# A decoder trunk whose engine orders are drawn up on the scheduler's time line model in place of its default model

## The chip, the cores and the metric

The kernel runs on one core of one Trainium2 chip. The metric is the time of one execution on the device in microseconds (us), the median of several runs. Beside it there is one profiled execution, taken by the hardware profiler, from which all rows of traces come.

## The reference

The reference is a trunk of two decoder layers on 256 tokens of width 1024, in float32. Each layer is a feed-forward half step, a mixer, and another feed-forward half step; every stage adds to the residual stream `h`:

```
for layer in range(2):
    h = h + 0.5 * swiglu(rmsnorm(h, ffn1_norm), w_gate, w_up, w_down)     # 1024 -> 2816 -> 1024
    hn = rmsnorm(h, mix_norm)
    h = h + (mixer_a(hn, qkv, w_o) if layer == 0 else mixer_b(hn, w_q, w_o, shared k and v))
    h = h + 0.5 * swiglu(rmsnorm(h, ffn2_norm), ...)
    if layer == 0: shared = k and v of rmsnorm(h, kv_norm)
return rmsnorm(h, final_norm)

swiglu(h) = (silu(h @ w_gate) * (h @ w_up)) @ w_down
```

Both mixers are attention with 16 heads of 64 and a rotary embedding on 16 of the 64 dimensions. Mixer a merges three dilated causal windows, which on 256 tokens comes to one softmax with a mask that counts how often a key is seen. Mixer b is block-sparse, and with 256 tokens in one block of 256 it is plain causal attention.

## The kernel before

**Numbers.** Each float32 operand is split into a high and a low part of type fp32r: the high part is a copy by ScalarE (ACT; `wh`, L156, L307, and L94 for activations), the low part is what is left, a subtraction by VectorE (DVE; `wl`, L157, L309, and L90/L92 for activations). TensorE (PE) multiplies high by high, high by low and low by high. All weights, 174 MB, are streamed from memory once by DMAs that SyncE (SP) issues, into four raw buffers (`rawp`); the parts go into eight buffers for each of `wh` and `wl`.

**Stages.** `ffn("f10")`, mixer a, `ffn("f20")`, `ffn("f11")`, mixer b, and `f21`, whose down projection is written by `down_last`. The first feed-forward has an `opening` (L162 to L174) that brings in the weights and the input in small pieces. In a feed-forward, `products_t` (L193, L196) makes gate and up, `close` (L352 to L356) activates them, `down_t` multiplies by the down weights. `Norm` sums squares (L226 and L229 on ACT, L230 on GpSimd, POOL) and ends in a column of factors (`finish`, L235 on PE).

**A mixer.** `projections` multiplies the normed input by the q, k and v weights (`product`, L182, L184, L186) in six segments. Beside it stand the steps of attention, which go by pairs of heads, 0 to 7:
- the projected q and k are evacuated (L612), rotated (L485 to L488), turned by PE (`qt`, L601) and split into `qkh` and `qkl`;
- scores (`s_a3` is pair 3 of mixer a; L506, two heads on two halves of the array), the masked minimum on DVE (L514), exponentials on ACT (L520), a reciprocal (L525) and a scaling (L527; on POOL, for the last two pairs on DVE);
- turn: the weights of attention are transposed by PE (`pt`, L532) and split into `pT`, high part on ACT (L94), low part on DVE (L90);
- values: `po` (L546, L548) from `pT` and `vs` (L92, L94), evacuated half by ACT (L550) and half by an add on DVE (`o`, L555), and split again into `oT`.

At the end `out_t` (L453 to L455) multiplies the eight `oT` by the output weights into four accumulators, and adds them to the stream `hT` (L472); `norm.scale` then makes the next stage's `x`. PSUM has five accumulators (`accp`), of which `out_t` holds four, and three buffers for transposes and scores (`trp`); `pT` has two buffers.

**What sets the order.** The author writes the program in an order that an `Agenda` works out by hand-given costs and due times: each projection step counts 0.68, each output step 0.72, and a step of attention is written when its due time has come. For the last pairs, for example:

```
def ending(at):
    return [(at + 2.6 * i + wait, step, 4 + i) for i in range(4) for wait, step in ((0.0, "t"), (2.3, "v"))]
```

The rest is left to the framework: inside `tile.TileContext` a scheduler takes the written program with its dependences and decides in which order each engine gets its instructions, by a model of what each of them costs. Engines then run their own lists in order and wait for each other by semaphores. The change is in the call that opens this context:

## Time and profile before

| | |
|---|---|
| median of 3 runs | 990.88 us (990.67 to 990.91) |
| the profiled execution | 990.92 us |
| its span (first to last instruction) | 989.1 us |
| time around the span | 1.8 us |
| granted TensorE clock, mean | 1.00 |
| PE busy | 976.2 us of 989.1 |
| DVE, ACT, POOL busy | 729.4, 586.1, 170.1 us |
| read from memory | 173.99 MB, 177 GB/s over the span |

In rows of the trace the first number is the start in us after the span's start, the second the duration; then come the engine, the line of the kernel, the operation, the tiles (out<-in), the shape, and in brackets the idle time before it and the instruction that ended it. PE's matmuls overlap, so two neighbours are told apart by their starts, not by their durations. In groups of instructions the busy total and the mean in ns stand behind the first bar, the idle time ahead of the group behind the second.

### The profile page before, as it was taken

Reading aid. Unit: us, or ns where it says so; the run is one execution under the profiler, and the core shown is the slowest. Engines: PE = TensorE matmul, PEld = TensorE weight load, DVE = VectorE, ACT = ScalarE, POOL = GpSimd, SP = SyncE. Lnnn points to the kernel's source line nnn. Section 1 sums busy time; section 2 is a strip of 40 time slices with the busy share of each in tenths; the row PEclk is TensorE's granted clock in tenths of the full one; section 3 lists DMA queues with packets and bytes.
Section 4 is the critical chain, followed back from the end, with each engine's and each line's share of the span. In section 5 each row is a group of like instructions: output and inputs, shape, how many; then the busy total and the mean of one; then the engine's idle time right before and its main releaser. Section 6 shows DMA issues by size and latency. Waiting matters only on the chain.

```text
span 989.1 us, 15227 instructions
## 1 busy us (share of the span) xinstructions
PE 976.2 (99%) x5652; PEld 849.5 (86%) x5652; DVE 729.4 (74%) x1291; ACT 586.1 (59%) x1073; POOL 170.1 (17%) x194
## 2 busy tenths in 40 slices
PE   8999999999999999999999999999999999999997
PEld 5888888888889888888888888888888998888886
DVE  6987866677887788776678877656678878888642
ACT  7656654467776665655456566545577756665531
POOL 3211111122302211110112111101143022111000
PEclk9999999999999999999999999999999999999999
DMA  9776565655433566565655665665534345655611
GB/s 303 246 256 204 169 210 185 213 171 171 128 117 125 171 187 206 178 200 181 212 171 172 198 191 185 202 202 190 194 128 128 120 141 173 207 174 201 202 62 43
DMA packets 152395, 176.03 MB, mean 178 GB/s; under 512 B 3584, under 2 KB 140288, under 8 KB 152320
## 3 DMA queue, kind: packets, MB, share of 16 engines
q1 hardware_dynamic: 151600, 174.24, 55.1%
q8 instruction: 44, 0.72, 0.3%
q10 hardware_dynamic: 720, 0.82, 0.2%
q14 instruction: 31, 0.25, 0.1%
HBM read 173.99 MB, written 1.05 MB: 177 GB/s over the span
## 4 chain that ended last, share of the span: by engine, by line
PE 68%; DVE 2%; ACT 2%; issue 1%; POOL 0%; POOLq 0%; ACTq 0%; DVEq 0%
PE f_g L193 12%; PE f_u L193 12%; PE dn_f L193 8%; PE f_u L196 6%; PE f_g L196 6%; PE dn_f L196 4%; PE dn_f_d L186 2%; PE dn_f_d L182 2%; PE dn_f_d L184 2%; PE q_b L182 1%; PE kv_b L182 1%; PE q_b L186 1%; PE kv_b L186 1%; PE kv_b L184 1%; PE q_b L184 1%
## 5 line engine op out<-in xcount | busy, mean ns | idle before, releaser
L193 PE MATMUL f_g<-x_n,wh_f_g 128*128 128x512 f32 x688 | 180.1, 394 | 0.0
L193 PE MATMUL f_u<-x_n,wh_f_u 128*128 128x512 f32 x688 | 177.3, 390 | 0.0
L193 PEld LDWEIGHTS f_u<-x_n,wh_f_u 128*128 128x128 f32 x688 | 129.1, 188 | 27.3
L193 PEld LDWEIGHTS f_g<-x_n,wh_f_g 128*128 128x128 f32 x688 | 124.1, 189 | 22.7
L355 POOL TENSOR_TENSOR j_f_u<-j_f_u,r_n 128x256 f32<-128x256 f32 x88 | 77.6, 884 | 377.9 <-DVE j_f_u L337 355.5
L193 PE MATMUL dn_f<-act_f,wh_f 128*128 128x512 f32 x528 | 126.5, 391 | 0.0
L157 DVE TENSOR_TENSOR wl_f_u<-raw_f_u,wh_f_u 128x1024 fp32r<-128x1024 f32 x86 | 119.6, 1393 | 1.5 <-ACT wh_f_u L156 1.4
L157 DVE TENSOR_TENSOR wl_f_g<-raw_f_g,wh_f_g 128x1024 fp32r<-128x1024 f32 x86 | 103.6, 1235 | 15.1 <-PE f_g L196 10.7
L193 PEld LDWEIGHTS dn_f<-act_f,wh_f 128*128 128x128 f32 x528 | 96.8, 188 | 18.6
L157 DVE TENSOR_TENSOR wl_f<-raw_f,wh_f 128x1024 fp32r<-128x1024 f32 x72 | 81.8, 1153 | 35.6 <-ACT wh_f L156 26.7
L196 PE MATMUL f_u<-x_n,wl_f_u 128*128 128x256 f32 x688 | 103.3, 283 | 0.0
L196 PE MATMUL f_g<-x_n,wl_f_g 128*128 128x256 f32 x688 | 102.9, 282 | 0.0
L196 PEld LDWEIGHTS f_g<-x_n,wl_f_g 128*128 128x128 f32 x688 | 96.5, 190 | 6.3
L156 ACT ACTIVATE wh_f<-raw_f 128x1024 fp32r<-128x1024 f32 x72 | 67.3, 979 | 49.4 <-PE dn_f L193 27.1
L156 ACT ACTIVATE wh_f_g<-raw_f_g 128x1024 fp32r<-128x1024 f32 x86 | 89.4, 1049 | 11.2 <-issue 6.0
L156 ACT ACTIVATE wh_f_u<-raw_f_u 128x1024 fp32r<-128x1024 f32 x86 | 86.6, 1047 | 15.2 <-PE f_g L193 10.9
L196 PEld LDWEIGHTS f_u<-x_n,wl_f_u 128*128 128x128 f32 x688 | 91.6, 192 | 0.0
L230 POOL TENSOR_TENSOR ss_n<-ss_n,sq_n 128x256 f32<-128x256 f32 x42 | 41.9, 999 | 244.2 <-ACT sq_n L229 243.3
L94 ACT ACTIVATE act_f<-j_f_g 128x256 fp32r<-128x256 f32 x88 | 36.5, 417 | 72.1 <-DVE j_f_g L356 71.8
L353 ACT ACTIVATE j_f_g<-j_f_g 128x256 f32<-128x256 f32 x88 | 36.8, 418 | 67.1 <-DVE j_f_g L352 66.6
L196 PEld LDWEIGHTS dn_f<-act_f,wl_f 128*128 128x128 f32 x528 | 68.1, 191 | 2.8
L196 PE MATMUL dn_f<-act_f,wl_f 128*128 128x256 f32 x528 | 69.0, 283 | 0.0
(220 smaller groups left out, 1702.3 us busy)
## 6 DMA issues: line engine op xcount, KB each, us to landing
raw_f_g<-in_ffn_w_gate_dram SPq DMA_DIRECT2D x43, 1024.0 KB, 5.4
raw_f_u<-in_ffn_w_up_dram SPq DMA_DIRECT2D x43, 1024.0 KB, 5.3
raw_f<-in_ffn_w_down_dram SPq DMA_DIRECT2D x24, 1024.0 KB, 5.1
raw_f_d<-in_ffn_w_down_dram SPq DMA_DIRECT2D x11, 1024.0 KB, 4.9
raw_f<-in_ffn_w_down_dram SPq DMA_DIRECT2D x12, 768.0 KB, 4.5
raw_qka<-in_a_w_qkv_dram SPq DMA_DIRECT2D x16, 512.0 KB, 4.3
raw_va<-in_a_w_qkv_dram SPq DMA_DIRECT2D x4, 1024.0 KB, 5.1
raw_ao<-in_a_w_o_dram SPq DMA_DIRECT2D x4, 1024.0 KB, 4.9
```

The source lines that it names most:

```text
L94: nc.scalar.activation(hi, src, AF.Copy, scale=scale)
L156: nc.scalar.activation(wh, r, AF.Copy)
L157: nc.vector.tensor_sub(wl, r, wh.bitcast(F32))
L182: nc.tensor.matmul(ac, xh, wh, start=first, stop=False)
L184: nc.tensor.matmul(ac, xh, wl, start=False, stop=False)
L186: nc.tensor.matmul(ac, xl, wh, start=False, stop=last)
L193: nc.tensor.matmul(ac, wh, flat(x), start=first and i == 0, stop=False)
L196: nc.tensor.matmul(ac[:, :S], wl, x[:, 0, :], start=False, stop=last and i == len(ws) - 1)
L230: nc.gpsimd.tensor_tensor(self.ss, self.ss, sq, op=ALU.add)
L353: nc.scalar.activation(g, g, AF.Silu)
L355: nc.gpsimd.tensor_tensor(u, u, norm.row, op=ALU.mult)
```

## The change

```
@@ -756,7 +756,7 @@
-    with tile.TileContext(nc) as tc:
+    with tile.TileContext(nc, schedule_with_timeline_sim=True) as tc:
         trunk(tc, args, out)
```

The scheduler draws up the orders on its time line model, where it used its default model. The written program is the same, and so are the instructions; what differs is the order on each engine. In the built programs, POOL's order is the same in both. On SP, only the three late constants' loads (L137 to L139) move: from behind the eighth weight load of the first feed-forward and later to a place between the loads of `raw_f10_g2` and `raw_f10_u2`. PE, DVE and ACT differ in the opening, in both mixers and where the next feed-forward begins; in the steady feed-forward and down stages PE's order is the same and a few weight splits swap places. In the mixers, projections stand earlier and steps of attention later and more scattered:

| on PE, both mixers | before | after |
|---|---|---|
| uninterrupted groups of scores (L506) | 16 | 31 |
| matmuls of scores that stand as a pair of heads | 96 pairs | 41 pairs, 110 single |
| groups of values (L546, L548) | 18 | 35 |
| groups of transposes (L532, L601) | 34 | 45 |

At the end of mixer a, DVE's built order after the change is as follows; mixer b has the like:

```
L525 Reciprocal ls_a7
L527 TensorScalarPtr sm_a7_1 (2 instructions)
L157 TensorTensor wl_f20_g0_0<-raw_f20_g0,wh_f20_g0_0
L157 TensorTensor wl_f20_g0_4<-raw_f20_g0,wh_f20_g0_4
L157 TensorTensor wl_f20_u0_0<-raw_f20_u0,wh_f20_u0_0
L157 TensorTensor wl_f20_u0_4<-raw_f20_u0,wh_f20_u0_4
L90 TensorTensor pT_a5_0<-pt_a5_0,pT_a5_0
L555 TensorTensor o_a4<-po_a4,o_a4 (2 instructions)
L90 TensorTensor pT_a5_1<-pt_a5_1,pT_a5_1
L90 TensorTensor oT_a4<-o_a4,oT_a4
```

In `out_t`'s part of PE's order, the last four `oT` (4 to 7) stand after the change with all 24 matmuls each, one `oT` behind the other; before, each accumulator takes the last three `oT` together, 18 matmuls, before the next one does.

## The prediction

> **What bounds the kernel now.** I read the page first, then the waits of TensorE (PE), then busy time by stage, and last the time lines of single stretches.

> ```profile
> span 989.1 us, 15227 instructions
> ...
> PE 976.2 (99%) x5652; PEld 849.5 (86%) x5652; DVE 729.4 (74%) x1291; ACT 586.1 (59%) x1073; POOL 170.1 (17%) x194
> ...
> PEclk9999999999999999999999999999999999999999
> ```

> PE is busy 99% of the span, at a full granted clock throughout. So the end can move in three ways only: PE waits more or less, its matmuls follow each other less or more tightly, or its clock falls. The multiset of PE work is unchanged by this change. The waits of PE and its busy time by stage say how much there is to win:

> ```profile
> PE f_g L193 <- ACT wh L171: 1.7, 2, 1.0
> PE po_a L546 <- DVE vs_a L92: 1.5, 1, 1.5
> ...
> PE po_b L546 <- DVE pT_b L90: 1.0, 1, 1.0
> ```

> ```profile
> 0.00:25.00 25.00, 20.89 (x96) 14.56 (x97) 16.23 (x24) 18.52 (x32) 9.24 (x14) 1.00 0.96 304
> 25.00:200.00 175.00, 175.00 (x1004) 154.46 (x1003) 134.81 (x204) 100.73 (x170) 27.94 (x29) 1.00 0.66 212
> ...
> 282.00:305.00 23.00, 21.37 (x173) 20.47 (x172) 17.50 (x30) 16.05 (x31) 0.00 (x0) 1.00 0.36 107
> ...
> 765.00:800.00 35.00, 33.85 (x275) 32.38 (x274) 29.07 (x71) 26.29 (x61) 6.25 (x8) 1.00 0.30 93
> ```

> (Columns: window, length, busy PE, PEld, DVE, ACT, POOL, granted clock, DMA share, GB/s.) The feed-forward stage at 25 to 200 us has no idle PE time. PE idles in the opening (25.00 - 20.89 = 4.1 us, with the DMA engines 96% busy), at the end of mixer a (1.6 us) and in the window around the end of mixer b (1.15 us). All that a better order can win by waits is those, and the opening's are mostly the first load and the first weights.

> A second cost is hidden in "busy". Here are a scores group in the middle of mixer a, a group of transposes, and the values matmuls (po, L546/L548) at mixer b's end:

> ```profile
> 212.84 0.39 PE L184 MATMUL v_a<-wl_va,x_n 128*128 128x512 f32 x1
> 213.06 0.39 PE L186 MATMUL v_a<-wh_va,x_n 128*128 128x512 f32 x1
> 213.38 0.33 PE L506 MATMUL s_a<-qkh_a 64*128 64x128 f32 x2
> ...
> 213.94 0.28 PE L506 MATMUL s_a<-qkl_a,qkh_a 64*128 64x256 f32 x2
> 214.06 0.28 PE L506 MATMUL s_a<-qkh_a,qkl_a 64*128 64x256 f32 x2
> 214.27 0.50 PE L182 MATMUL v_a<-wh_va,x_n 128*128 128x512 f32 x1
> 214.61 0.39 PE L184 MATMUL v_a<-wl_va,x_n 128*128 128x512 f32 x1
> ```

> ```profile
> 247.38 0.60 PE L601 MATMUL qt_a<-ident,rt_a 128*128 128x128 f32 x4
> 247.91 0.33 PE L506 MATMUL s_a<-qkh_a 64*128 64x128 f32 x2
> ```

> ```profile
> 774.25 0.39 PE L546 MATMUL po_b<-pT_b,vs_b 128*128 128x256 f32 x1 [1.02 <-DVE pT_b L90]
> ...
> 775.11 0.62 PE L532 MATMUL pt_b<-ident,sm_b 128*128 128x128 f32 x4
> ```

> Between projection matmuls the pitch is 213.06 - 212.84 = 0.22 to 0.23 us. The one ahead of the scores takes 213.38 - 213.06 = 0.32 and the one behind them 214.61 - 214.27 = 0.34, and the last score pair 214.27 - 214.06 = 0.21 where the pair ahead of it takes 0.12. So entering and leaving a scores group costs 0.09 + 0.11 + 0.10 = 0.30 us. Four transposes take 0.53 where four pitches of 0.11 make 0.44: 0.09 a group. The seven po matmuls between 774.25 and 775.11 take 0.86, where three pitches of 0.12 and four of 0.06 make 0.60; as 0.1 of it is the restart after a wait, I take 0.19 for each values group.

> **The change part by part.** It alters no operation, only the orders that the scheduler writes. I compared the built orders of both kernels, engine by engine, and priced each stretch that differs.

> *Opening.* ACT's squares move ahead of weight splits, and the three late constants (0.95 MB) move ahead of one early weight load: 0.95 MB at the 304 GB/s above is 3.1 us more ahead of that load in a saturated stretch. Earlier squares release the norm column earlier. I take -0.5 us (bounds -0.7 to +1.5).

> *Switches in the mixers.* Uninterrupted scores groups go from 16 to 31, values groups from 18 to 35, transpose groups from 34 to 45: 15 x 0.30 = 4.5, 17 x 0.19 = 3.2, 11 x 0.09 = 1.0, together 8.7. Scores also lose their partner: the "x2" rows above are two heads on two halves of the array in one 0.12 us slot; before, all 96 pairs run so, after only 41, with 110 matmuls single. At worst each single costs a slot of its own (55 x 0.12 = 6.6); at best nothing. I take the whole at +8.5 alone, and +7 because about 1.5 of it falls into the stalls below. Bounds +4 to +14.

> *Middle of the mixers.* Before, projection matmuls lie between a pair's scores, its turn and its values. After, in mixer a the scores of pair 3, the turn and values of pair 2 and the scores of pair 4 stand in one cluster with 1.6 us of PE work between s_a3 and po_a2. ACT has the four exponentials of pair 3 ahead of the parts that po_a2 reads:

> ```profile
> L520 ACT ACTIVATE sm_a<-sm_a,nm_a 128x256 f32<-128x256 f32 x16 | 7.9, 496 | 0.0
> L94 ACT ACTIVATE pT_a<-pt_a 128x384 fp32r<-128x384 f32 x16 | 6.9, 482 | 0.1
> L520 ACT ACTIVATE sm_a<-sm_a,nm_a 128x128 f32<-128x128 f32 x16 | 6.3, 396 | 12.9 <-DVE nm_a L514 12.9
> ...
> L520 ACT ACTIVATION_READ_ACCUMULATOR sm_a<-sm_a,nm_a 128x1 f32 x32 | 6.0, 188 | 0.0
> ```

> 2 x (496 + 396 + 2 x 188) + 482 = 3.0 us, about 1 more (estimate) for the mins of its first head (0.285 + 0.418 below) and a hand-over: 4.0 - 1.6 = 2.4 us of new wait. The like cluster in mixer b gives 1.2. Bounds 0 and 5 for both.

> *End of the mixers.* This is the largest term. VectorE (DVE) before puts one feed-forward weight split (wl, L157) between the attention steps of two pairs:

> ```profile
> 286.11 1.22 DVE L157 TENSOR_TENSOR wl_f_g<-raw_f_g,wh_f_g 128x1024 fp32r<-128x1024 f32 x1
> ...
> 291.68 1.23 DVE L157 TENSOR_TENSOR wl_f_g<-raw_f_g,wh_f_g 128x1024 fp32r<-128x1024 f32 x1 [0.24 <-ACT wh_f_g L156]
> ```

> After, four of these stand in one block behind the last scales and ahead of the lo part of pT_a5 and the add of o_a4. PE's po_a5 waits for both: for its operand, and for its accumulator (out_t holds four of five). The durations:

> ```profile
> L90 DVE TENSOR_TENSOR pT_a<-pt_a,pT_a 128x384 fp32r<-128x384 f32 x16 | 8.1, 549 | 0.2 <-ACT pT_a L94 0.2
> L514 DVE CUSTOM_DVE_ANT_0 sm_a<-s_a,masks 128x256 f32<-128x256 f32 x16 | 6.7, 418 | 0.0
> L555 DVE TENSOR_TENSOR o_a<-po_a,o_a 64x256 f32<-64x256 f32 x16 | 6.6, 415 | 4.8 <-ACT o_a L550 4.7
> ...
> L514 DVE CUSTOM_DVE_ANT_0 sm_a<-s_a,masks 128x128 f32<-128x128 f32 x16 | 4.6, 285 | 0.1
> L157 DVE TENSOR_TENSOR wl_f_g<-raw_f_g,wh_f_g 128x1024 fp32r<-128x1024 f32 x3 | 3.7, 1223 | 1.4 <-ACT wh_f_g L156 1.4
> ...
> L92 DVE SCALAR_TENSOR_TENSOR vs_a<-v_a,c_n,vs_a 128x256 fp32r<-128x256 f32 x8 | 3.5, 478 | 1.0 <-ACT vs_a L94 1.0
> ...
> L525 DVE RECIPROCAL ls_a<-ls_a 128x2 f32<-128x2 f32 x16 | 2.6, 163 | 3.7 <-ACT sm_a L520 3.6
> ...
> L527 DVE TENSOR_SCALAR sm_a<-sm_a,ls_a 128x256 f32<-128x256 f32 x4 | 1.4, 348 | 0.0
> L527 DVE TENSOR_SCALAR sm_a<-sm_a,ls_a 128x128 f32<-128x128 f32 x4 | 1.1, 288 | 0.1
> ```

> From the scores of the last head (s_a7_1) on, DVE's order is: two mins 0.7, two reciprocals 0.3, two vs 0.95, four scales 1.27, two pT 1.1, four wl 4.9, pT_a5 0.55, two adds 0.83, pT_a5 0.55: 11.1 us. (Ends of neighbours overlap by some 0.05 to 0.1, which takes off about 0.9; the wait for the last exponentials adds about as much.) PE's order between the same two points holds 6.1 us. The difference is 5 us if DVE arrives on time and 6 with DVE a little late at s_a7_1; I take 6.0. In mixer b the same block stands between the turns of pairs 4 and 5, and the first half delays po_b4 too: 5 to 8.5, taken 7.0. The 1.6 and 1.15 us of idle time that the windows show there now go. Bounds for both blocks together: 5 (half the block covered by slack) and 16.

> *Start of the next feed-forward.* Before, out_t ends with its last three steps column by column, so hT's first columns are added while PE still has 5 us of work. After, PE runs oT_4 to oT_7 each over all columns, and DVE does all eight adds ahead of the lo part of the first x:

> ```profile
> 304.99 0.75 DVE L472 TENSOR_TENSOR hT<-ot_ao,hT 128x256 f32<-128x256 f32 x2
> 305.99 0.89 DVE L92 SCALAR_TENSOR_TENSOR x_n<-hT,gT,x_n 128x256 fp32r<-128x256 f32 x2 [0.24 <-ACT x_n L94]
> ```

> PE then waits for the last two adds (0.75), the first lo part (0.45) and two hand-overs (0.24 each, the idle time in the second row): 1.7 us, in both mixers. Bounds 0.5 and 2.5 each.

> *Sum.* Mixer a: 2.4 + 6.0 + 1.7 - 1.6 = +8.5. Mixer b: 1.2 + 7.0 + 1.7 - 1.15 = +8.75. Switches +7.0, opening -0.5: +23.75. The profiled execution took 990.92 us (span 989.1, 1.8 around it), the median is 990.88, so both give **1014.6 us**. The steady feed-forward and down stages keep PE's order and I cost them at nothing; what hides their few swapped weight splits is that DVE is busy 135 of 175 us there; without that cover a swap costs one split, 1.2 us.

> **The rivals.** *A: the cover holds.* The scheduler may have drawn up orders in which DVE and ACT run far enough ahead that blocks and clusters cost nothing. For it: DVE's 74%. Against: DVE's eleven microseconds at the end of mixer a begin with mins that need PE's own last scores, so DVE cannot be ahead there. Then only switches remain, +8.5 - 0.5: 999 us.

> *B: faster.* The new order removes the idle time at the mixers' ends (-1.6 - 1.15) and 0.5 in the opening, and its switches fall into idle time that is left: 987.6. It is decided at po_5: if DVE's block ends no more than 1.6 us after PE gets there, the new wait is no longer than the old one. Against: 11 us of DVE beside 6 of PE.

> *C: the clock falls too.* The first row of PE's time line:

> ```profile
> 1.44 3.59 PE L116 MATMUL busy<-fill 128*128 128x512 bf16 x8 [1.44 <-DVE fill L113]
> ```

> Eight matmuls of 512 columns in 3.59 us, 0.45 each, twice the later 0.23: after an idle start PE runs at half speed for some 3.6 us, a loss of 3.59 - 8 x 0.23 = 1.75. Behind the 1.0 and 1.5 us waits above, the clock stays at 9. If a new wait is long enough to bring it down, each such wait costs 1.75 more; with three (po_a5, po_b4, po_b5), +5.3: 1020 us. [...] I expect the block to come in pieces, with matmuls between, and keep the lower value.

> *D: no change.* Stalls small and waits removed balance the switches: 991.

> **How the numbers follow.** Forecast 0.64, A 0.13, C 0.13, B 0.07, D 0.03. The terms' bounds, their distances added as squares, give about 1006 to 1024 for the forecast; A pulls the low end to 998 and C the high end to 1028. About 0.2% (2 us) is what a measurement tells from no change: faster 0.07, same 0.03, slower 0.90.

> **What would show it.** In the profile after: PE waits on pT and o (L90, L555) of 5 to 8 us around each mixer's end, with four L157 rows of DVE in a block just ahead; a wait of PE on x_n or hT (L92, L472) of 1 to 2 us at f20's and f21's start; PE idle 15 us more than before, its busy time 5 to 10 us more at the same instruction count; PEclk at 9, or below 9 by the mixers' ends (C). The prediction is wrong if these windows show PE waits under 3 us in all, if the steady stages lengthen, or if the opening moves by over 2 us.

## The result, and the profile after

The kernel takes 1015.7 us (median of 5 runs, 1012.66 to 1017.86) where it took 990.88 (5 runs, 990.41 to 991.23): a ratio of 1.0249, 95% interval 1.0237 to 1.026. It is slower by 24.8 us; 23.7 were forecast. The total came out nearly right by luck: two of its terms were wrong and offset each other, as the rows show. The page of the profile after, first its head:

```profile
span 1013.9 us, 15253 instructions
...
PE 992.5 (98%) x5652; PEld 862.5 (85%) x5652; DVE 712.4 (70%) x1291; ACT 579.3 (57%) x1073; POOL 158.9 (16%) x194
...
PEclk9999999999899999999999999999999999999999
```

PE has the same 5652 matmuls, is busy 16.3 us longer and idle 8.5 us longer (21.4 against 12.9). One slice of the 40 of the clock shows an 8, the eleventh (253 to 279 us). The waits of PE in the kernel after (us in total, times, longest):

```profile
PE f_g L193 <- DVE x_n L92: 5.5, 3, 2.5
PE pt_a L532 <- DVE pT_a L90: 2.5, 1, 2.5
PE qt_a L601 <- DVE qkl_a L90: 1.9, 1, 1.9
PE pt_b L532 <- DVE pT_b L90: 1.6, 1, 1.6
```

The two waits of before at the mixers' ends (vs_a, pT_b) are gone. In their place stand one in the middle of mixer a (qkl_a), one at each mixer's end (pT) and one at the start of each feed-forward behind a mixer (x_n); with three of 0.3 us (po_a and po_b for o, s_a for qkl_a) that makes 12.4 us. Busy time by stretches around these waits shows what the waits list doesn't (the last three columns are granted clock, DMA share, GB/s):

```profile
260.00:272.00 12.00, 9.85 (x42) 7.92 (x40) 5.80 (x20) 4.42 (x16) 5.10 (x7) 0.72 0.36 113
300.00:312.00 12.00, 9.21 (x66) 8.77 (x65) 8.63 (x14) 6.62 (x14) 0.00 (x0) 0.86 0.56 175
322.00:332.00 10.00, 7.07 (x38) 5.67 (x37) 10.00 (x16) 6.70 (x17) 6.36 (x7) 1.00 0.37 117
795.00:806.00 11.00, 9.11 (x65) 8.66 (x64) 9.56 (x19) 7.72 (x16) 0.00 (x0) 0.84 0.59 193
818.00:829.00 11.00, 8.45 (x39) 6.75 (x38) 10.02 (x16) 6.88 (x18) 6.35 (x7) 0.84 0.34 107
```

In four of the five the clock is below 1. In stretches cut where it changes, as further down, it is at 1.00 or at 0.50; so a mean of 0.72 over 12 us is 2 x 0.28 x 12 = 6.7 us at half speed, the others 3.4, 3.5 and 3.5: together 17.1 us, which cost PE 8.6 us. The row from 322 has a wait of the same length as the row from 818, and no loss of clock (1.00 against 0.84). PE's rows at the end of mixer a and at the first clock drop:

```profile
259.74 0.28 PE L506 MATMUL s_a<-qkh_a,qkl_a 64*128 64x256 f32 x2
261.89 0.70 PE L601 MATMUL qt_a<-ident,rt_a 128*128 128x128 f32 x4 [1.87 <-DVE qkl_a L90]
...
266.27 0.63 PE L182 MATMUL v_a<-wh_va,x_n 128*128 128x512 f32 x1
266.70 0.63 PE L184 MATMUL v_a<-wl_va,x_n 128*128 128x512 f32 x1
...
270.40 0.39 PE L182 MATMUL v_a<-wh_va,x_n 128*128 128x512 f32 x1
270.63 0.39 PE L184 MATMUL v_a<-wl_va,x_n 128*128 128x512 f32 x1
...
304.77 0.55 PE L532 MATMUL pt_a<-ident,sm_a 128*128 128x128 f32 x3 [2.49 <-DVE pT_a L90]
305.61 0.48 PE L546 MATMUL po_a<-pT_a,vs_a 128*128 128x256 f32 x2 [0.30 <-DVE o_a L555]
...
324.80 0.47 PE L193 MATMUL f_g<-x_n,wh_f_g 128*128 128x512 f32 x1 [2.55 <-DVE x_n L92]
```

Behind the wait that ends at 261.89 two projection matmuls stand 0.43 us apart; at 270.40 they are back at 0.23. The block that was forecast stands on DVE just ahead of the wait that ends at 304.77. The first two rows are a smaller one, ahead of the wait that ends at 261.89:

```profile
258.47 2.77 DVE L309 TENSOR_TENSOR wl_ao<-raw_ao,wh_ao 128x1024 fp32r<-128x1024 f32 x2 [1.69 <-ACT wh_ao L307]
261.16 0.68 DVE L90 TENSOR_TENSOR qkl_a<-qt_a,qkh_a 128x512 fp32r<-128x512 f32 x1
...
296.17 0.29 DVE L514 CUSTOM_DVE_ANT_0 sm_a<-s_a,masks 128x128 f32<-128x128 f32 x1 [0.17 <-PE s_a L506]
...
299.62 2.35 DVE L157 TENSOR_TENSOR wl_f_g<-raw_f_g,wh_f_g 128x1024 fp32r<-128x1024 f32 x2
301.89 2.35 DVE L157 TENSOR_TENSOR wl_f_u<-raw_f_u,wh_f_u 128x1024 fp32r<-128x1024 f32 x2
304.16 0.55 DVE L90 TENSOR_TENSOR pT_a<-pt_a,pT_a 128x384 fp32r<-128x384 f32 x1
304.63 0.83 DVE L555 TENSOR_TENSOR o_a<-po_a,o_a 64x256 f32<-64x256 f32 x2
```

There two splits of the output weights stand ahead of qkl_a, which frees the buffer that PE's next transposes (qt_a) need; the other two of the three buffers hold pair 3's scores.

The length of each section, from the start of its first matmul to that of the next section's, says where the time is:

| section | before, us | after less before |
|---|---|---|
| f10 with the opening | 192.68 | -0.85 |
| mixer a | 117.15 | +14.39 |
| f20 and f11 | 369.64 | +0.66 |
| mixer b | 116.61 | +9.08 |
| f21 | 125.29 | +1.58 |
| last down product and what follows | 66.30 | -0.05 |

By cause: waits of PE +9.9 (12.4 less the 2.5 of before), clock +8.6, opening -0.85; the 7.2 that are left of 24.8 I put down to switches between kinds of matmuls in the mixers, of which only one kind is measured by itself below. The opening's -0.85 is that of one execution: in the seven kernels below that leave the opening to the model it is -1.29 to +0.09. The runs differ by the clock as well: the run of 1012.66 us had a mean granted clock of 0.994, that of 1017.86 us 0.988. Over the span that is about 6 us more of lost clock, for 5.2 us more time.

### The profile page after: what moved, and what is told of

It reads as the page before. It is cut to its first block, busy times and chain, and to the rows that moved or that the text cites. A ratio compares the mean times of both kernels' runs of the same rounds, so it can differ in the third digit from the quotient of the medians.

```text
span 1013.9 us, 15253 instructions
## 1 busy us (share of the span) xinstructions
PE 992.5 (98%) x5652; PEld 862.5 (85%) x5652; DVE 712.4 (70%) x1291; ACT 579.3 (57%) x1073; POOL 158.9 (16%) x194
## 4 chain that ended last, share of the span: by engine, by line
PE 94%; DVE 3%; ACT 1%; issue 1%; DMA 1%; SPq 0%; POOL 0%; POOLq 0%; ACTq 0%; DVEq 0%
PE f_g L193 16%; PE f_u L193 16%; PE dn_f L193 12%; PE f_u L196 8%; PE f_g L196 8%; PE dn_f L196 6%; PE dn_f_d L184 2%; PE dn_f_d L186 2%; PE dn_f_d L182 2%; PE qk_a L182 2%; PE qk_a L184 2%; PE qk_a L186 1%; PE s_b L506 1%; PE s_a L506 1%; PE v_a L182 1%; PE v_a L184 1%
## 5 line engine op out<-in xcount | busy, mean ns | idle before, releaser
L193 PE MATMUL f_g<-x_n,wh_f_g 128*128 128x512 f32 x688 | 181.8, 395 | 5.5 <-DVE x_n L92 5.5
L193 PE MATMUL f_u<-x_n,wh_f_u 128*128 128x512 f32 x688 | 179.4, 391 | 0.0
L193 PEld LDWEIGHTS f_u<-x_n,wh_f_u 128*128 128x128 f32 x688 | 128.8, 188 | 26.5
L193 PEld LDWEIGHTS f_g<-x_n,wh_f_g 128*128 128x128 f32 x688 | 124.4, 189 | 29.6 <-issue 5.4
L355 POOL TENSOR_TENSOR j_f_u<-j_f_u,r_n 128x256 f32<-128x256 f32 x88 | 71.4, 812 | 388.9 <-DVE j_f_u L337 363.0
L193 PE MATMUL dn_f<-act_f,wh_f 128*128 128x512 f32 x528 | 126.5, 391 | 0.0
L157 DVE TENSOR_TENSOR wl_f_g<-raw_f_g,wh_f_g 128x1024 fp32r<-128x1024 f32 x86 | 104.5, 1245 | 19.3 <-PE f_g L196 9.3
L193 PEld LDWEIGHTS dn_f<-act_f,wh_f 128*128 128x128 f32 x528 | 96.9, 188 | 18.6
L157 DVE TENSOR_TENSOR wl_f_u<-raw_f_u,wh_f_u 128x1024 fp32r<-128x1024 f32 x86 | 104.2, 1239 | 2.6 <-ACT wh_f_u L156 1.8
L336 ACT ACTIVATE j_f_g<-f_g 128x256 f32<-128x256 f32 x88 | 32.9, 374 | 127.1 <-PE f_g L196 124.9
L157 DVE TENSOR_TENSOR wl_f<-raw_f,wh_f 128x1024 fp32r<-128x1024 f32 x72 | 80.2, 1145 | 35.9 <-ACT wh_f L156 25.4
L156 ACT ACTIVATE wh_f_g<-raw_f_g 128x1024 fp32r<-128x1024 f32 x86 | 86.9, 1047 | 18.7 <-PE f_g L193 9.0
L156 ACT ACTIVATE wh_f_u<-raw_f_u 128x1024 fp32r<-128x1024 f32 x86 | 87.2, 1046 | 16.6 <-PE f_g L193 10.7
L156 ACT ACTIVATE wh_f<-raw_f 128x1024 fp32r<-128x1024 f32 x72 | 67.5, 978 | 47.4 <-issue 24.8
L230 POOL TENSOR_TENSOR ss_n<-ss_n,sq_n 128x256 f32<-128x256 f32 x42 | 37.3, 887 | 240.8 <-ACT sq_n L229 239.6
L90 DVE TENSOR_TENSOR act_f<-j_f_g,act_f 128x256 fp32r<-128x256 f32 x88 | 38.1, 434 | 26.9 <-ACT act_f L94 26.9
```

Of the source, the lines that this page charges most:

```text
L90: nc.vector.tensor_sub(lo, src, hi.bitcast(F32))
L156: nc.scalar.activation(wh, r, AF.Copy)
L157: nc.vector.tensor_sub(wl, r, wh.bitcast(F32))
L193: nc.tensor.matmul(ac, wh, flat(x), start=first and i == 0, stop=False)
L230: nc.gpsimd.tensor_tensor(self.ss, self.ss, sq, op=ALU.add)
L336: nc.scalar.activation(s, ac[:, S:], AF.Copy)
```

## The experiments

Theory P: PE's new order in the mixers makes the loss, by waits, switches and the clock drops that waits bring. Rival H: the blocks of weight splits on DVE and ACT make it, whatever PE's order. Orders were held with edges that fix only who is issued first on an engine, no waits (the lines added shift the line numbers in these kernels' rows by 4 to 24):

```
def behind(ins, prev):          # same engine: ins is issued after prev
    tc.add_manual_dep(ins, prev.name, DependencyInfo(NoSync, DATA), reason="order")
def pin(engine, lo, hi):        # the engine's instructions written between two marks keep the written order
    seen = [i for i in nc.cur_bb.bb.instructions[lo:hi] if i.engine == engine.engine]
    for prev, ins in zip(seen, seen[1:]): behind(ins, prev)
```

**PE's order or the helpers'.** Three kernels hold PE to the written order in a part of the program; before, PE stood in nearly that order everywhere.

```
+    pin(nc.tensor, <start of each mixer>, <end of the step f == 2 behind it>)       # pe_written_mixers
+    pin(nc.tensor, <everything but those stretches>)                                # pe_written_elsewhere
+    pin(nc.tensor, <start of each mixer>, <end of agenda.run(projections())>)       # projections_written
```

> The kernel after, with PE held to the written order from the start of each mixer to the first step of the next feed-forward; DVE, ACT and SP keep what the time line model gives them. Theory P (PE's new order in the mixers makes the loss: waits, switches and a slower clock): 990 to 993 us, granted clock back at 1.00, scores in 16 groups, no wait of PE over 2 us behind the opening. Rival H (the blocks of weight splits on DVE and ACT make it, whatever PE's order): 1000 us or more, with PE waiting on pT or o at the mixers' ends.

> The kernel after, with PE held to the written order everywhere but in the mixers and the first step of the feed-forward behind each. Theory P: 1014 to 1018 us, as after, plus the 0.9 us that the opening had won; granted clock 0.99. A theory by which the opening or the steady stages matter: under 1010 us.

> The kernel after, with PE held to the written order in the projections' part of both mixers only; the output product, its tail and the start of the next feed-forward are the model's. If mixer middle and mixer end add up: the middle's wait (2.15 us), its slower clock (3.4 us) and most of the 7.6 us of switches go, the end's waits stay (2.8 and 1.9 us, then 2.9 and 2.55 us at the feed-forward's start) with two to four clock drops of 1.7 us: 1000 to 1005 us. If the end's waits come from the middle (everything late there): under 996 us.

Measured: 993.18 us with the mixers pinned, just above the range of P (before on the same chip 991.25; ratio 1.0024, interval 1.0014 to 1.0033), 1016.51 with all but the mixers pinned (1.025, 1.0235 to 1.0266), 1002.08 with only the projections' part pinned (1.0108, 1.0093 to 1.0124). So PE's order in the mixers carries nearly the whole loss, and it comes off in two parts: about 13.6 us (1015.7 - 1002.08) with the projections' part pinned, 9 more (1002.08 - 993.18) with the output product and the feed-forward's start pinned too. The parts are not two separate places: with only the projections' part pinned, the 2.5 us wait at mixer a's end goes as well, though that end was left to the model, while the waits on x_n stay (2.5 us each). H is right only for the rest. With the mixers pinned mixer a is as long as before (-0.12) and mixer b 3.64 us longer, by one wait that the helpers' order makes, and a clock drop behind it (3.4 us at half clock from 750.6 us on):

```profile
PE qt_b L617 <- DVE pT_b L103: 1.9, 1, 1.9
```

**The block of splits.** Each of the four splits at a mixer's end is queued behind the output step of one of the last four pairs, the high part behind ACT's evacuation, the low part behind DVE's add (L555).

```
 def pieces_of(name, raw, k, n):
-            nc.scalar.activation(wh, r, AF.Copy)
-            nc.vector.tensor_sub(wl, r, wh.bitcast(F32))
+            hi = nc.scalar.activation(wh, r, AF.Copy).ins
+            lo = nc.vector.tensor_sub(wl, r, wh.bitcast(F32)).ins
+            if name in ("f20_g0", "f20_u0", "f21_g0", "f21_u0"):
+                evac, add = <those of pair 4 + 2 * (name[4] == "u") + j // 4>
+                behind(hi, evac); behind(lo, add)
```

> The kernel after, with the four weight splits ahead of each feed-forward behind a mixer (high parts on ACT, low parts on DVE) queued one behind each of the last four pairs' output steps instead of in one block; PE's order is left to the model. Theory P with the clock: the waits at the mixers' ends (2.8 and 1.9 us) go and with them two drops of the clock of 1.7 us each: 1007 to 1009 us. Without a clock effect: 1010 to 1012 us. If the block is not what PE waits for there: 1014 to 1018 us.

Measured: 1009.34 us (1.0184, 1.0169 to 1.0199), 6.4 less than after. In the profiled execution there is no clock drop at either mixer's end or behind it any more, only the one in the middle of mixer a (6.8 us at half speed). The waits, though, have not gone but been cut up:

```profile
303.41 0.48 PE L563 MATMUL po_a<-pT_a,vs_a 128*128 128x256 f32 x2 [0.90 <-DVE o_a L573]
305.50 0.38 PE L471 MATMUL ot_ao<-oT_a,wh_ao 128*128 128x256 f32 x1 [0.15 <-DVE oT_a L103]
317.30 0.74 PE L470 MATMUL ot_ao<-oT_a,wh_ao 128*128 128x256 f32 x4 [1.22 <-ACT oT_a L107]
318.96 0.39 PE L471 MATMUL ot_ao<-oT_a,wh_ao 128*128 128x256 f32 x1 [0.93 <-DVE oT_a L103]
```

They add up to 3.2 us between 300 and 320 us, where after has 2.8 there and 2.9 at f20's start. Mixer a became 2.8 us shorter and mixer b 2.0. So the block was a cause of the long wait, but most of the gain is the clock that the shorter waits do not bring down: 17.1 - 6.8 us less at half speed are 5.1 us of PE's time, of 7.2 between the two profiled executions. The time of 1009.34 us lies between the two ranges that were expected.

**The order at the feed-forward's start.** DVE is held to the written order where out_t ends.

```
+        lo = traced()
         for i in range(KD // 2):
             ...
                 nc.vector.tensor_add(hT[:, d, :], accs[i][:, j * S:(j + 1) * S], hT[:, d, :])
                 norm.scale(d)
+        pin(nc.vector, lo, traced())
```

> The kernel after, with DVE held to the written order where out_t ends (the adds of two columns, then the low parts of their x, then the next two) instead of all eight adds ahead of the first low part. If that order makes the 2.55 us wait at the start of f20 and of f21: 5.1 us less in waits, and 1.7 to 3.4 us less if the clock drops behind them: 1007 to 1010 us. If PE then waits as long for the next x: 1013 us or more.

> The kernel after with both repairs: the four splits spread over the last four pairs, and the first x ahead of the later adds. Theory P: both gains add up, 999 to 1002 us; what is left over before is the switches (7 to 8 us), the 2.1 us wait in the middle of mixer a and its drop of the clock. If the two waits stand in for one another: 1005 us or more.

Both missed. The first takes 1019.38 us (1.0286, 1.0269 to 1.0303), the second, with the spread splits too, 1019.1 (1.028, 1.0266 to 1.0294): the repair makes it slower. DVE's rows of the first:

```profile
319.96 0.42 DVE L486 TENSOR_TENSOR hT<-ot_ao,hT 128x256 f32<-128x256 f32 x1
320.95 0.48 DVE L105 SCALAR_TENSOR_TENSOR x_n<-hT,gT,x_n 128x256 fp32r<-128x256 f32 x1 [0.58 <-ACT x_n L107]
...
335.64 0.41 DVE L486 TENSOR_TENSOR hT<-ot_ao,hT 128x256 f32<-128x256 f32 x1
```

The first x is there 3.2 us earlier (f20's first matmul starts at 321.58 instead of 324.80), but the adds now stand behind the x ahead of them, which costs 0.58 us for ACT's high part alone, and the last of the eight adds starts at 335.6 us where after had all eight done by 324.3. As PE's order finishes all four accumulators within the last 2.9 us, adds first and x behind them was the better order for DVE. What makes these waits is PE's order from the output product on: with all of it in written order (pe_written_mixers) there is no wait on x_n, with only the projections' part in written order they stay.

**Filling a wait.** Eleven extra matmuls of ones run where PE waits for the first x; the first real matmul clears their accumulator.

```
+                if name in ("f20", "f21"):
+                    prev = <the last matmul written so far>
+                    for _ in range(11):
+                        ins = nc.tensor.matmul(acs[0][0], fill[:, :P], fill, start=True, stop=True).ins
+                        behind(ins, prev); prev = ins
```

> The kernel after, with eleven extra matmuls (512 columns of ones, 2.4 us at full clock) between the last output matmul of each mixer and the first matmul of the next feed-forward, into an accumulator that the first real matmul then clears. PE is busy in the wait instead of idle; nothing else changes. If idle time takes the clock down: no drop behind f20's and f21's start, 1.7 to 3.4 us less than after: 1011 to 1014 us, granted clock 0.992 to 0.995. If the clock falls for another reason (the amount of work or power): time as after or a little more, 1015 to 1018 us.

Measured: 1012.76 us (1.0224, 1.0206 to 1.0242). The fill takes 2.55 us and the clock stays at 1.00 behind both feed-forward starts. This agrees with idle time as the cause, but doesn't settle it: in this profiled execution the drops at the mixers' ends were missing too, though the waits there (2.5 and 1.6 us) were not, and one lay in the opening instead. The grid described below says why: there each of these waits is divided over two stretches, with no more than 1.42 us of idle time in either.

**The clock by itself.** In the kernel before, PE waits behind column pairs of the down products for a chain of small operations (on POOL in the first kernel, shorter and on DVE in the second).

```
 down_t, behind the adds of a column pair's first column:
+    g = sp.tile([P, P], F32, tag="gate", ...)
+    nc.gpsimd.tensor_tensor(g, hT[:, d, :P], hT[:, d, :P], op=ALU.add)      # nc.vector in short_gates
+    for _ in range(<0 to 13>): nc.gpsimd.tensor_tensor(g, g, g, op=ALU.add)
+    nc.tensor.matmul(trt(...)[:, :1], g, mean, start=True, stop=True)
```

> The kernel before, with nine waits of PE put into its steady down stages, one behind each of the first three column pairs of the three down products: PE waits for a chain of 1, 2, 3, 4, 5, 7, 9, 11 and 14 short operations on POOL that begins when DVE has made its add. If a wait of about 2 us takes the clock down, as the waits of 1.9 to 2.8 us after did and that of 1.5 us before didn't: each gate of 2 us or more is followed by some 3.4 us at half clock, each shorter one by none. If a whole idle stretch of 3.4 us is needed: only the gates of 3.4 us and more are.

> The kernel before, with nine shorter waits of PE at the same places as the longer ones, each behind DVE's add and a chain of 1, 2, 3, 4, 1, 2, 3, 4 and 5 small operations on DVE: waits of about 1 to 2.5 us. If the clock falls from a wait length on: none below that length, all above, and the length lies between 1.5 and 1.95 us. If the fall depends on where the wait lies against a window that runs by itself: drops and no drops at like lengths.

Measured: 1066.77 us and 1039.11 us. PE's rows of three of the long gates, and the stretches from these waits on:

```profile
150.43 0.59 PE L351 MATMUL gt_f<-mean,gate_f 128*128 128x1 f32 x2 [1.95 <-POOL gate_f L348]
...
171.07 0.59 PE L351 MATMUL gt_f<-mean,gate_f 128*128 128x1 f32 x2 [3.29 <-POOL gate_f L350]
...
193.83 0.38 PE L351 MATMUL gt_f<-mean,gate_f 128*128 128x1 f32 x2 [3.88 <-POOL gate_f L350]
```

```profile
147.00:157.00 10.00, 8.05 (x40) 6.87 (x39) 4.76 (x8) 5.01 (x8) 1.13 (x2) 0.83 0.64 207
170.00:180.00 10.00, 8.93 (x34) 7.49 (x35) 2.30 (x5) 2.98 (x5) 2.63 (x3) 0.66 0.33 105
193.00:203.00 10.00, 9.17 (x42) 7.75 (x43) 3.22 (x5) 2.82 (x4) 2.12 (x4) 0.83 0.33 105
```

Waits of 1.95, 3.29 and 3.88 us are followed by 3.4, 6.8 and 3.4 us at half clock (2 x 0.17 x 10, 2 x 0.34 x 10): the loss comes in units of 3.4 us, each worth 1.7 us of PE's time, and grows with the wait only roughly. Two gates of the same length in the second kernel, and stretches around them:

```profile
150.22 0.28 PE L351 MATMUL gt_f<-mean,gate_f 128*64 128x1 f32 x2 [1.94 <-DVE gate_f L348]
...
489.23 0.28 PE L351 MATMUL gt_f<-mean,gate_f 128*64 128x1 f32 x2 [1.94 <-DVE gate_f L348]
```

```profile
147.32:150.73 3.41, 1.47 (x12) 1.24 (x11) 3.02 (x7) 2.12 (x5) 0.00 (x0) 1.00 0.78 273
150.73:154.14 3.41, 3.41 (x9) 2.63 (x8) 2.16 (x3) 0.62 (x2) 1.19 (x1) 0.50 0.19 56
485.24:488.65 3.41, 2.05 (x15) 1.76 (x13) 1.93 (x4) 2.01 (x2) 0.00 (x0) 1.00 0.83 258
488.65:492.06 3.41, 2.83 (x14) 2.37 (x14) 3.41 (x7) 2.33 (x6) 2.05 (x2) 1.00 0.15 49
492.06:495.48 3.42, 3.42 (x24) 3.18 (x23) 1.79 (x4) 2.01 (x2) 0.12 (x1) 1.00 0.72 232
```

The first is followed by 3.4 us at half clock, the second by none. So there is no single length from which the clock falls, at least not between 1.5 and 2.6 us: where the wait lies decides with it. That a whole idle stretch of 3.4 us is needed is refuted by the same 1.94 us.

```profile
320.40:323.82 3.42, 1.86 (x16) 1.65 (x14) 3.42 (x8) 3.30 (x6) 0.00 (x0) 1.00 0.62 217
323.82:327.23 3.41, 2.10 (x10) 1.52 (x10) 3.41 (x6) 3.41 (x11) 2.54 (x3) 1.00 0.00 0
...
818.75:822.16 3.41, 1.37 (x8) 1.22 (x8) 3.41 (x7) 3.41 (x9) 1.56 (x2) 1.00 0.00 0
822.16:825.58 3.42, 3.42 (x11) 2.55 (x10) 3.42 (x5) 2.52 (x8) 3.17 (x4) 0.50 0.51 153
```

A stretch's length less PE's busy time is its idle time. The gate at 150.2 has its 1.94 us in one stretch, and the next is at half clock; the gate at 489.2 has them divided into 1.36 and 0.58, and the clock stays. f20's start divides its waits into 1.56 and 1.31 us and loses nothing; f21's has 2.04 us in one stretch and loses the next. Counted over all fourteen executions, from the clock's first rise to the last matmul: of 36 stretches at full clock with 1.6 us or more of idle time, 35 were followed by half clock (the exception has 1.89 us, in projections_written), and of 3995 with less, two (1.12 us in pe_written_elsewhere and 1.52 in model_outside). The way back came with nearly unbroken work: a stretch at half clock with 0.06 us of idle time or less was always followed by full clock, one with 0.32 us or more never (from 0.21 to 0.29 both occur). This fits the longer gate that costs less: the 3.88 us lie as 1.39 and 2.49 in two stretches, with no idle time behind them, and one stretch is lost; the 3.29 lie as 3.08 and 0.21, and behind the 0.21 the clock stays down for a second stretch. This is a count, not a test of its own: no run moves a wait against the grid.

**The price of a switch.** In the kernel before, the scores of a pair are written in two steps, 0.3 apart on the agenda, so that a projection or output step lies between; the minima follow the second.

```
-            for t, seg in enumerate(segs):                       # scores(p): both halves
+            scores_of(p, 0, hi, lo, ps, b)                       # first 128 tokens
+            agenda.after(0.3, scores_rest, p, hi, lo, ps, b)     # second 128 tokens, then the minima
```

> The kernel before, with the scores of each pair written in two steps (first 128 tokens, then the second), at least one projection or output step apart, so that PE has 32 groups of scores instead of 16, all still two heads at a time. At 0.30 us a group: 990.9 + 16 x 0.30 = 995.7 us, with up to 1.4 us more where the later softmax lengthens the wait at a mixer's end. If a switch costs nothing that isn't there anyway: 991 us.

Measured: 994.75 us (1.0035, 1.0022 to 1.0047), +3.6 us where 4.8 were expected. The net hides two terms. PE's rows of one pair:

```profile
212.89 0.39 PE L186 MATMUL v_a<-wh_va,x_n 128*128 128x512 f32 x1
213.21 0.33 PE L510 MATMUL s_a<-qkh_a 64*128 64x128 f32 x2
...
214.03 0.39 PE L184 MATMUL v_a<-wl_va,x_n 128*128 128x512 f32 x1
214.26 0.40 PE L186 MATMUL v_a<-wh_va,x_n 128*128 128x512 f32 x1
214.58 0.39 PE L510 MATMUL s_a<-qkh_a 64*128 64x256 f32 x2
...
215.48 0.39 PE L184 MATMUL v_a<-wl_va,x_n 128*128 128x512 f32 x1
```

From the matmul ahead of a group to the second one behind it take 1.14 and 1.22 us; less the two projection matmuls (0.45) that is 0.69 and 0.77, together 1.46, where the undivided group of before takes 1.10 (from 213.06 to 214.61, less the same). A further group costs 0.36 us, more than the 0.30 forecast; sixteen make 5.8. In exchange the waits of 1.5 and 1.0 us at the mixers' ends shrank to 0.2 each.

**Versions that might beat both.** The first takes the model's orders outside the mixers and the exact orders of before (PE, DVE, ACT) inside; the second is the kernel before with one weight split at each mixer's end held behind pair 4's second pT.

```
+    behind(<ACT wh_ao_3_0>, <ACT pT_a4_1 high>); behind(<DVE wl_ao_3_0>, <DVE pT_a4_1 low>)      # two_splits_later
+    behind(<ACT wh_f21_g0_0>, <ACT pT_b4_1 high>); behind(<DVE wl_f21_g0_0>, <DVE pT_b4_1 low>)
```

> The time line model everywhere but from each mixer's start to the first step of the feed-forward behind it; there PE, DVE and ACT are held to the very orders of the kernel before. If the opening's 0.9 to 1.2 us (seen in after and in three of its variants) is real and the mixers come out as before: 989.9 us against 991.1 before, granted clock as before. If the mixers' ends shift against DMA or POOL: 991 us or more.

> The kernel before, default model, with one weight split (high part on ACT, low part on DVE) at each mixer's end moved behind the low part of the second pT of pair 4: wl_ao_3_0 in mixer a, wl_f21_g0_0 in mixer b. If the waits of 1.5 and 1.0 us there are the 1.2 us split ahead of vs and pT: about 1 us less in each mixer, and no clock drop behind mixer a's wait in any execution: 989.0 to 989.8 us against 991.2. If the split is needed there all the same (the output product waits for it later) or ACT's exponentials come last: 990.8 us or more.

The first gives 991.7 us (1.0009, 1.0 to 1.0018), no gain: in its profiled execution f10 is 0.57 us shorter, but the wait of 1.5 us on vs_a, as in before, is followed by a clock drop (3.4 us at half clock from 285.6 us on). The drop is not the whole reason, as the three of its runs with a mean clock of 1.00 take 991.15 to 991.58 us; in mixer b PE waits 2.1 us (po_b 1.2, ot_bo 0.9) where before has 1.0. The second gives 989.7 us against 991.0 (0.9986, 0.9977 to 0.9996): faster than both, by 0.14%. The waits on vs_a and pT_b have gone but for 0.2 us, and a smaller one is new:

```profile
PE po_a L570 <- DVE o_a L579: 0.9, 1, 0.9
```

## Why the prediction came out

**Right.** Bound and place: PE is the limit, and the loss lies in the mixers and where the next feed-forward begins, not in the steady stages. The opening: -0.5 forecast, -0.85 measured, in a term that varies by more than a microsecond. The waits that would go: 2.75, measured 2.5. Switches: +7.0, against 7.2 as what is left over, so argued rather than measured; the one price tested by itself, that of a scores group, was forecast at 0.30 and is 0.36. Rival A (the cover holds) falls by the 12.4 us of waits and by the total, B by the sign, and D with it.

**Right in size, wrong in cause: mixer a's middle.** 2.4 us were forecast for po_a2, which was to wait for pT behind ACT's exponentials of pair 3. Measured are 1.87 + 0.28 us, but po_a2 does not wait at all: the first is qt_a, held up by two weight splits on DVE ahead of qkl_a, the second the scores behind it. That the sizes agree is luck.

**Wrong, too high: the end of the mixers.** The step that set 11.1 us of DVE beside 6.1 of PE gave 6.0 and 7.0 us; measured are 2.79 and 1.89. Three parts of it failed. Durations were added where neighbours start before the last has ended; the same work took from 296.17 to 305.46, 9.3 us. The compensating wait for the last exponentials didn't come. And the second pT_a5 was counted, though po_a5 can start without it. PE on its side had 6.8 us of work, not 6.1, between the two places. The releaser was another one too: PE stopped a step earlier, at a transpose that needs the buffer that pT_a5 was to free. In mixer b the first half of the block did not delay po_b4 at all: PE's first wait there is the one that ends at 800.73. So the sign "PE idle 15 us more" did not come either; it is 8.5.

**Wrong, too low: the clock.** The forecast took nothing for it, and rival C, at 0.13, 5.3 us; measured are 8.6. The cause that rival C named was at work, in four places instead of three and two of them others (the middle of mixer a, f21's start). The step that failed is "I expect the block to come in pieces, with matmuls between, and keep the lower value": that waits cut into pieces would leave the clock up was the author's estimate, and no row of before shows how long a wait has to be; its own two, of 1.5 and 1.0 us, lost nothing. Here waits of 1.5 us (model_outside) to 2.6 us brought the clock down, some of them and some not, so the measurement decides against a least length of a wait: about 1.6 us of idle time within one stretch of the grid went with the fall. The price of one drop came out as forecast: 1.75 us, taken from the first row of PE, against 1.7 us for each 3.4 us at half clock.

**Wrong in the cause: the feed-forward's start.** 1.7 us each were forecast, 2.94 and 2.55 measured, and put down to DVE doing eight adds ahead of the first x. first_x_first shows that this order is no fault; PE's order from the output product on is what makes the wait.

**Missed:** mixer b's middle (1.2 forecast, no wait there). The sum of the blocks is 8.3 us too high and the clock 8.6 too low; with either term right and the other wrong, the forecast would have missed by some 8 us. That it did not is luck. Two smaller slips of the working: the values group comes to 0.86 - 0.60 - 0.10 = 0.16 us, not 0.19, and the distances added as squares give about 1005 to 1023 us, not 1006 to 1024.

**Open:** whether the clock falls between 1.5 and 1.6 us of idle time in a stretch, where both occur, and why the two stretches with 1.12 us and with 1.89 us go against the count; and what a values and a transpose group cost, as only the scores were tested by themselves.

## What to carry to other kernels

With the matrix engine busy 99% of the time, an order that left more and longer waits on it was paid for twice here: once for the wait and once, in some executions, for the clock behind it (1.7 us for each 3.4 us at half clock). So one wait of two microseconds can do more harm than several short ones that lie apart: at mixer a's end the 2.49 us of after brought a drop, the four waits of 0.15 to 1.22 us there and behind it in splits_spread none. When stretches on two engines are set against each other, add start-to-start times, not durations, and look which buffer is freed by the last step, since the engine may stop there earlier than at the operand. Before an order on a helper engine is blamed for a wait, hold the bound engine's order still and look whether the wait remains.

## What the hardware showed that was not expected

- A wait of PE of 1.5 to 2.6 us can halve the granted clock right behind it: 1.50 us did in one kernel and 1.49 us did not in the profiled execution of before; 1.94 us did and did not within one execution; 2.55 us did at f21's start and did not at f20's. What the fourteen profiled executions set apart is PE's idle time within one stretch of a grid of 3.413 us: with 1.6 us or more 35 of 36 stretches at full clock were followed by half clock, with less 2 of 3995.
- The clock comes back after 3.4 us or a multiple (3.4, 6.8, in the longest gates 10.2 us, part of them still within the wait), so each 3.4 us cost 1.7 us of matmul time, whatever the length of the wait.
- The same order and the same work lose a different amount of clock in each run: the five of the kernel after spread over 5.2 us, with mean clocks from 0.988 to 0.994, which is about 6 us of clock. The grid's place, another one in each of the thirteen profiled executions, may be the reason; one execution of each kernel doesn't show it.
